# A Hyena, RWKV-7 and mixture-of-experts layer: the recurrent part in lockstep of four heads, issued in the order of a list scheduler

## The chip, the core and the metric

The program runs on one core of one Trainium2 chip. Time is device microseconds (us) of the whole program: one launch reads all inputs from memory and writes the output. The core has TensorE (PE; its weight loads are shown apart as PEld), VectorE (DVE), ScalarE (ACT), GpSimd (POOL) and SyncE (SP), which here only issues DMAs.

## The reference, cut to what matters

The layer works on 512 latent tokens (behind 256 context tokens) of 1024 channels, all in float32:

```
cols  = rmsnorm(x) * (1 + m[1]) + m[0]  @ w_in            # Hyena 1536, RWKV 1792, gates 2048 columns
y_hy  = hyena_branch(hy_cols) @ hy_proj                   # a long convolution
S <- S (diag(w) + a^T b) + v^T k ;  y = S r               # RWKV-7, 8 heads of 64, forwards and backwards,
                                                          # state carried over from the context tokens
y_rw  = (groupnorm(y_fwd + y_bwd) + bonus) * gate         # then @ rw_proj
mixed = (sigmoid(g_hy) * y_hy + sigmoid(g_rw) * y_rw) @ w_out
x     = x + m[2] * rmsnorm(mixed)
x     = x + m[5] * rmsnorm(experts(rmsnorm(x)))           # 16 experts, each takes its 64 best tokens
```

## The kernel before

The program runs through stages: modulation and norm, Hyena with all projections (to 322 us of the profiled execution), the **recurrent part** (322 to 784), the merge with the gates, output projection and router (784 to 939), and the experts, whose weights stream in from memory until the end.

In the recurrent part tokens are cut into chunks of 64. For one head and direction a batch is four chunks, and there are three: the context's (0) and the latents' two (1, 2). A head pair ("group", 4 of them) goes through these stages per batch: `pieces` (decays and scaled keys; two small float32r products "pus" per direction, L810, then a scan along time, L816), `scores` (L882), `inverses` and `levels` (the inverse of a triangular 64x64 matrix; the 16x16 blocks go through DRAM, L889 to L964, then small products, L973), `values` (values transposed on PE into UV, keys into BT), `steps` (L1043 to L1110) and at the end `epilogue`. In `steps` a chunk costs a chain: `p1` on PE (L1063, L1070), its copy X1 on DVE, `p2` on PE (L1076), the copy into UV, `p3` on PE (L1085), and the new state; the output `ya` (L1094, L1097) hangs beside it. The next chunk needs the state. Groups follow one another; two strings, ORD0 and ORD1, say how one group's steps are mixed with the preparation of the next, and the compiler's scheduler with priorities sets the final order.

Two kinds of other work stand between these products. The **gates** (L711 to L722) are 16 column tiles of `w_in`, each a 512 KB load and 16 matmuls of 256 tokens against the normalised input `hraw`, which is kept in SBUF. **Zeros** fill up: `pump` (L288) issues one matmul of zeros after `p1`, `p2` and `p3`, and each bank of `levels` first takes two (L941). The decay weights `ur` of a group come by one DMA on ACT's queue (the first group's early, "ahead", L686); ACT and POOL split them into `us`.

Each float32 matmul leaves two records in the trace, and counts below are of records. Raw weights pass through `raw_tile`s of 4 KB a partition, of which there are NRAW = 3; the gates use them, and the merge for `w_hy_proj`, `w_rw_proj` and `w_out`, where ACT (L212) and DVE (L216) split each into two parts.

## Time and profile before

| | us |
|---|---|
| median of 2 timed runs (1876.72 and 1878.56) | 1877.64 |
| span of the profiled execution, which is its own time too | 1886.6 |
| recurrent part in it | 322 to 784 |
| PE busy in the recurrent part | 444.13 of 462.00 |
| merge | 784 to 850 |

The page shows busy time of each engine over the span and in 40 slices; the stages above come from sums over windows of the trace and from its timeline. "PEclk" or the clock column is the share of full speed that TensorE was granted: 1.00 is 2.4 GHz, 0.50 is 1.2 GHz, and a mean between them says which part of the stretch each held.

### The profile page before, as it was taken

The numbers are of one execution on the slowest core, as the hardware profiler recorded it, in microseconds if no ns is written. First come the engines' busy times: TensorE is split into PE (matmuls) and PEld (weight loads), VectorE is DVE, ScalarE is ACT, GpSimd is POOL, SyncE is SP. The second block draws the span as 40 slices with busy tenths as digits, with TensorE's granted clock in tenths as the row PEclk, the third lists the DMA queues.
The fourth block names the chain that finished last, engine by engine and source line by source line (L and its number), as shares of the span: only waits on it lengthen the run. The fifth ranks groups of instructions, "written<-read, shape, count | busy, mean of one in ns | idle before, by whom it ended". The sixth has DMA issues, their size and how long they took to land.

```text
span 1886.6 us, 32798 instructions
## 1 busy us (share of the span) xinstructions
PE 1702.4 (90%) x14006; PEld 1107.5 (59%) x14006; DVE 681.9 (36%) x1520; ACT 434.5 (23%) x941; POOL 214.5 (11%) x255
## 2 busy tenths in 40 slices
PE   8898999999999999789599999889899898998985
PEld 3466786667666767668475545555455454554542
DVE  4765875867584742363500202002020020200203
ACT  3544531434453433333100000000000000000001
POOL 0534102422131300020000000000000000000000
PEclk5799999899999899999699999999999999999998
DMA  7255543433222221571799999999999999999995
GB/s 304 95 187 192 172 159 114 144 83 67 64 69 40 57 47 41 179 269 62 295 402 427 426 427 427 426 427 426 427 427 427 426 427 426 426 426 427 426 427 231
DMA packets 143292, 516.46 MB, mean 274 GB/s; under 512 B 83259, under 2 KB 87499, under 8 KB 118572
## 3 DMA queue, kind: packets, MB, share of 16 engines
q1 hardware_dynamic: 139824, 509.68, 68.8%
q10 hardware_dynamic: 3324, 4.70, 0.7%
q8 instruction: 110, 1.80, 0.4%
q14 instruction: 34, 0.28, 0.0%
HBM read 490.98 MB, written 23.36 MB: 273 GB/s over the span
## 4 chain that ended last, share of the span: by engine, by line
PE 39%; DMA 14%; DVE 3%; ACT 1%; issue 1%; POOL 0%; SPq 0%; DVEq 0%; ACTq 0%; POOLq 0%
PE ph L1425 17%; DMA exp_w<-in_exp_w 12%; PE py L1438 10%; PE px L1392 3%; PE pso L1460 3%; PE pht L249 1%; DVE hd L216 1%; PE po L1245 1%; PE po L1242 1%; PE po L1243 1%; ACT hT L212 1%; PE pl L1326 0%; PE pbq L1406 0%; PE pbp L1402 0%; DMA w_hy_proj<-in_hy_proj 0%
## 5 line engine op out<-in xcount | busy, mean ns | idle before, releaser
L1425 PE MATMUL ph<-exp_w,xe 128*64 128x256 f32 x4096 | 469.2, 380 | 26.7 <-DMA exp_w<-in_exp_w 26.7
L1425 PEld LDWEIGHTS ph<-exp_w,xe 128*64 128x64 f32 x4096 | 318.2, 137 | 194.8 <-issue 63.4
L216 DVE TENSOR_TENSOR hd<-ph,hd 128x256 f32<-128x256 f32 x64 | 27.2, 425 | 674.5 <-PE ph L1425 674.5
L1438 PE MATMUL py<-exp_w,hT 128*64 128x512 f32 x1024 | 236.8, 598 | 24.8 <-ACT hT L212 24.8
L1438 PEld LDWEIGHTS py<-exp_w,hT 128*64 128x64 f32 x1024 | 78.4, 136 | 138.7 <-issue 92.8
L719 PE MATMUL pgate<-hraw,w_gate 128*128 128x256 f32 x512 | 148.0, 409 | 0.7 <-ACT yo L212 0.3
L213 ACT ACTIVATE hd<-ph 128x256 f32<-128x256 f32 x64 | 24.5, 383 | 431.7 <-PE ph L1425 431.7
L719 PEld LDWEIGHTS pgate<-hraw,w_gate 128*128 128x128 f32 x512 | 90.6, 198 | 19.2 <-issue 3.8
L212 ACT ACTIVATE hT<-pht 128x256 f32<-128x256 f32 x64 | 24.5, 383 | 284.6 <-PE pht L249 284.6
L1392 PEld LDWEIGHTS px<-OH,xn 128*128 128x128 f32 x512 | 65.8, 197 | 23.4 <-issue 22.4
L1399 POOL COPY sel<-kcon 16x128 f32<-16x128 f32 x8 | 2.2, 283 | 609.4 <-PE pbq L1406 609.4
L1460 PE MATMUL pso<-ye,oT 128*128 128x512 f32 x128 | 68.7, 628 | 0.7 <-ACT ye L212 0.7
L1392 PE MATMUL px<-OH,xn 128*128 128x128 f32 x512 | 68.0, 282 | 0.9 <-DVE OH L223 0.9
L249 PE MATMUL pht<-kcon,hd 128*128 128x128 f32 x128 | 28.0, 301 | 36.1 <-DVE hd L216 35.9
L216 DVE TENSOR_TENSOR mo<-pso,mo 128x512 f32<-128x512 f32 x56 | 38.4, 691 | 39.3 <-PE pso L1460 39.3
L249 PEld LDWEIGHTS pht<-kcon,hd 128*128 128x128 f32 x128 | 12.9, 141 | 65.2 <-DVE hd L216 65.2
L882 PE MATMUL ps<-ar,bk 64*64 64x64 f32 (+1 forms) x512 | 46.5, 277 | 3.6 <-POOL bk L216 2.0
L882 PEld LDWEIGHTS ps<-ar,bk 64*64 64x64 f32 (+1 forms) x512 | 37.4, 177 | 16.5 <-POOL bk L216 5.0
L1443 DVE COPY ye<-py 64x512 f32<-64x512 f32 x16 | 11.1, 694 | 95.8 <-ACT ye L212 95.8
L216 POOL TENSOR_TENSOR mw<-mw 128x256 f32<-128x256 f32 x32 | 31.5, 1001 | 99.2 <-DVE mw L219 99.2
L288 PE MATMUL p<-zl 128*128 128x256 bf16 x140 | 40.0, 286 | 0.0
L212 ACT ACTIVATE sf<-st,fs 128x64 f32<-128x64 f32 x80 | 24.3, 341 | 49.6 <-DVE st L219 49.4
(396 smaller groups left out, 2549.7 us busy)
## 6 DMA issues: line engine op xcount, KB each, us to landing
exp_w<-in_exp_w SPq DMA_DIRECT2D x192, 2048.0 KB, 31.0
mw<-in_mod_w SPq DMA_DIRECT2D x48, 512.0 KB, 3.9
w_gate<-in_w_in SPq DMA_DIRECT2D x16, 512.0 KB, 4.9
w_h<-in_w_in SPq DMA_DIRECT2D x12, 512.0 KB, 4.1
w_c<-in_w_in SPq DMA_DIRECT2D x12, 512.0 KB, 5.6
g_d<-gt SPq DMA_DIRECT2D x16, 256.0 KB, 4.7
gg<-g_d SPq DMA_DIRECT2D x16, 256.0 KB, 5.5
w_o<-in_w_out SPq DMA_DIRECT2D x8, 512.0 KB, 5.3
```

The costliest lines, as they stand in the source:

```text
L212: return A.activation(out, in_, func, scale=scale, **kw)
L213: return A.activation(out, in_, func, bias=bias, scale=scale, **kw)
L216: e.tensor_tensor(out, a, b, op=op)
L249: TE.transpose(out, in_, ident[0:n, 0:n])
L288: mm(bk[:, 256:256 + NPW].rearrange("p (a b) -> p a b", b=P), zl, zw, start=True, stop=True)
L719: mm(pt[:, n:n + 256], w[:, k, :], hraw[:, k, n:n + 256], start=k == 0, stop=k == KD - 1)
L882: mm(pss[h][r, j * W:(j + 1) * W], BK[d](c)[HR[h], r], AR[d](c)[HR[h], 0:W], start=True, stop=True)
L1242: mm(pt, lhs[0][a], rhs[0][b], start=i == 0, stop=False)
L1392: mm(pt[:, k4 * P:(k4 + 1) * P], xn[:, n, k * P:(k + 1) * P], OH[:, n].rearrange("p a b -> p (a b)"), start=n == 0, stop=n == 3)
L1425: mm(ph[i][64 * hf:64 * hf + 64, 0:256], xe[:, k, 64 * e1:64 * e1 + 64], ws[i][:, k, hf * 256:(hf + 1) * 256], start=k == 0, stop=k == KD - 1)
L1438: mm(py[64 * dh:64 * dh + 64, :], hT_[:, i * P + 64 * hf:i * P + 64 * hf + 64], w2[:, 2 * hf + i, dh * 512:(dh + 1) * 512], start=b == 0 a ...
L1460: mm(pt, oT[:, n * P:(n + 1) * P], ye[:, dh * 512:(dh + 1) * 512], start=True, stop=True)
```

## The change

All engine calls of the recurrent part go through proxies of a class `Plan` and are only recorded. When the part is complete, `Plan.run` works out who depends on whom, gives each call a cost from a formula in the source, ranks it by the longest path behind it, schedules greedily per engine, and issues everything in that order under `manual_schedule`.

The stages are rewritten for two groups at a time (four heads, both directions): six units of work `(sg, bt)`, two groups `sg` alternating over three batches `bt`. An operation of `steps` is 8 matmuls of 64x64 in place of two times 4; the state update is two DVE operations. `scores` are 64x64 quadrants in two parts. No matmul of zeros is left in the part. `hraw` goes to DRAM (`h_d`) and comes back by quarters of 128 tokens; so each gate's weights are loaded four times, and a gate is 4 times 8 matmuls of 128 tokens. Values are transposed in the projection stage and stored (`vt_d`), and loaded by eight DMAs per unit. All four `us` are made at the start through one buffer, `gs`. NRAW is 2.

```diff
-NP1, NP2, NP3, NPW = 1, 1, 1, 256
-NRAW = 3
+NRAW = 2
+NMS, NAR, NBK, NUV, NBT = (3, 2), 3, 1, 2, 2
...
+class Plan:
+    def add(self, engine, what, f, a, k):
...
+            if what == "transpose" or min(rows, cols) > 64 or single:
+                place, t = None, 0.2 if what == "transpose" else size * (0.00055 if single else 0.00175) + 0.02
+            else:
+                place, t = (lhs.offset // lhs.ap[0][0], out.offset // out.ap[0][0]), 0.116 * size / 64
...
+        if what == "dma_start":
...
+            cost, lat = 0.07, 2.2 + size / (180e3 if run >= 512 else 60e3)
+        elif engine == "gpsimd":
+            cost, lat = 0.1 + 0.0023 * size, 0.1
+        elif engine == "scalar":
+            cost, lat = 0.15 + 0.0009 * size, 0.15
...
+    def run(self, tc):
...
+        for o in reversed(ops):
+            o["rank"] = o["cost"] + max((o["lat"] + ops[j]["rank"] for j in o["succ"]), default=0.0)
...
+                    o = min(rs, key=lambda o: (max(t, o["from"]), -o["rank"]))
...
+        with tc.manual_schedule():
+            for o in order:
+                for f, a, k in o["calls"]:
+                    f(*a, **k)
...
+                        vt = hp.tile([P, 6, P], F32, tag="vt", name=f"vt{m}")
+                        for a, b in ((0, 4), (4, 6)):
...
+                                transpose(pv[:, (i - a) * P:(i - a + 1) * P], cz[:, i * P:(i + 1) * P])
...
-            # the RWKV part's first group starts from these
-            ahead = raw_tile("ur0")[:, 0:2 * CT], raw_tile("k3c0")[:, 0:3 * CT]
-            A.dma_start(out=ahead[0], in_=I["ups"][0].rearrange("p i d f -> p (i d f)"))
...
-            w = filler[0](f"w_gate{i}").rearrange("p (k f) -> p k f", k=KD)
-            SY.dma_start(out=w, in_=w_in[o // P])
-            pt = pfl(f"pgate{i}")
-            for n in (0, 256):
-                for k in range(KD):
-                    mm(pt[:, n:n + 256], w[:, k, :], hraw[:, k, n:n + 256], start=k == 0, stop=k == KD - 1)
...
+            us = []
+            for g in range(4):
+                ur = buf("gs", [P, 2, 2, P])
+                A.dma_start(out=ur, in_=I["ups"][g])
+                u_ = rp.tile([P, 2, 2, P], F32R, name=f"us{g}")
+                act(u_, ur, AF.Copy)
...
+            def gates(i, q, h):
+                pt = sfl(f"pgate{q}{i}")
+                for n in range(4):
...
+                    w = turns("raw", raw_tile, NRAW).rearrange("p (k f) -> p k f", k=KD)
+                    SY.dma_start(out=w, in_=w_in[o // P])
+                    for k in range(KD):
+                        mm(pt[:, P * n:P * n + P], w[:, k, :], h[:, k, :], start=k == 0, stop=k == KD - 1)
...
+            for u in units:
+                pieces(u)
+                scores(u, 0)
+                inverses(u)
...
+            plan.run(tc)
```

ACT at the start of the recurrent part. `yo` is the last copy of the Hyena stage, `w1` and `ta` take the decays from `pus`, `E3` follows the scan. Before:

```order
L213 ACTIVATE cz3_2224<-pcl3_2225,par_67 128x512
L212 ACTIVATE yo3_2351<-pyo3_2346 128x256
L212 ACTIVATE us0_2388<-ur0_2280 128x512
L213 ACT_TABLE_LOAD
L213 ACTIVATE w1000_2396<-pus_2386,par_67 128x256
L213 ACTIVATE ta000_2397<-pus_2386,par_67 128x256
L213 ACTIVATE E3000_2416<-gs000_2405 128x256
```

With the change, where `gs_0` is the buffer that all four loads share with the first scan (`E3` reads it):

```order
L333 ACTIVATE yo3_2412<-pyo3_2407 128x256
L889 DMA gs_0_2439<-in_ups 128x512
L333 ACTIVATE us0_2441<-gs_0_2439 128x512
L889 DMA gs_0_2439<-in_ups 128x512
L313 ACT_TABLE_LOAD
L313 ACTIVATE w1_0_2470<-psmm_0_2472,par_67 128x256
L333 ACTIVATE us1_2446<-gs_0_2439 128x512
L313 ACTIVATE ta_0_2471<-psmm_0_2472,par_67 128x256
L889 DMA gs_0_2439<-in_ups 128x512
L333 ACTIVATE us2_2451<-gs_0_2439 128x512
L333 ACTIVATE us3_2456<-gs_0_2439 128x512
```

One load that lay ahead of the part has become four in turn, each behind the reader of the one before, and all four stand ahead of the first `E3`. (A second pair of `w1` and `ta` and the fourth DMA, which only repeat, are left out.)

PE in one step of the last group. `M`, `X`, `BT`, `AR` and `ar` are the prepared matrices, `st` the state, `psfl` and `pgate` a gate. Before:

```order
L1070 MATMUL p1313_7676<-st3120_7667,ar301_6490 64x64 x2
L1070 MATMUL p1313_7676<-st3121_7671,ar311_6527 64x64 x2
L288 LDWEIGHTS zl_61
L288 MATMUL p1313_7676<-zl_61 128x256
L719 MATMUL pgate13_8188<-hraw_173,w_gate13_8186 128x256 x2
L1076 MATMUL p2313_7687<-X1313_7675,xf1_2381 64x64 x4
```

With the change:

```order
L313 MATMUL psfl_0_2526<-hh_0_2525,raw_0_2527 128x128 x4
L313 MATMUL psst_1_2495<-st1_1_2508,AA_2_2509 64x64 x8
L313 MATMUL psya_0_2518<-AR_0_2510,st1_0_2507 64x64 x8
L313 MATMUL psfl_0_2526<-hh_0_2525,raw_1_2528 128x128 x4
L313 MATMUL psst_0_2494<-X1_0_2493,xf1_2436 64x64 x8
L313 MATMUL psfl_0_2526<-hh_0_2525,raw_1_2528 128x128 x4
```

Between `p1` and `p2` stood a matmul of zeros and two of a gate; now there stand matmuls of the other pair of groups and four of a gate at half the width.

SP at the stretch where a group's inverse comes back from DRAM. Before:

```order
L930 DMA X_d1_2374<-rb30_6109 64x16x16
L931 DMA X_d1_2374<-rt30_6110 64x16x16
L964 DMA X30_6267<-X_d1_2374 32x16x32 x4
L889 DMA N_d2_2373<-M320_6673 64x8x64
L722 DMA g_d_72<-gt10_8139 128x512
L715 DMA w_gate13_8186<-in_w_in 128x1024
```

With the change:

```order
L313 DMA g_d_72<-stg_0_2529 128x4x128
L313 DMA X_d1_2430<-rb_0_2482 128x16x16
L313 DMA X_d1_2430<-rt_0_2483 128x16x16
L313 DMA raw_0_2527<-in_w_in 128x1024
L313 DMA XX_0_2489<-X_d1_2430 32x16x32 x8
L313 DMA raw_1_2528<-in_w_in 128x1024
```

A gate's load, which waits for a raw buffer, now stands ahead of the eight loads that bring the inverse back.

## Rows read from the trace of the kernel before

**Rows 1.** The page's first line.

```profile
span 1886.6 us, 32798 instructions
```

**Rows 2.** Sums over windows: stretch, length, engines' busy time, granted clock, DMA share.

```profile
200.00:305.00 105.00, 103.19 (x505) 80.53 (x504) 76.17 (x96) 33.50 (x50) 15.41 (x15) 1.00 0.50 165
322.00:784.00 462.00, 444.13 (x6292) 316.69 (x6290) 265.14 (x773) 190.39 (x490) 104.57 (x152) 0.96 0.30 74
784.00:850.00 66.00, 52.28 (x210) 40.95 (x211) 41.64 (x47) 23.03 (x27) 13.96 (x9) 0.91 0.77 270
1228.00:1821.00 593.00, 534.49 (x3702) 305.40 (x3698) 72.33 (x159) 39.54 (x95) 3.20 (x4) 1.00 1.01 427
```

**Rows 3.** The same of one stretch of the recurrent part.

```profile
339.00:357.00 18.00, 15.63 (x76) 10.57 (x75) 12.79 (x36) 6.82 (x18) 7.16 (x9) 0.62 0.20 51
```

**Rows 4.** Timeline there: start, duration, line, count, idle before, its releaser.

```profile
341.27 0.68 PE L882 MATMUL ps<-ar,bk 64*64 64x64 f32 x28 [1.75 <-POOL bk L216]
```

**Rows 5.** Timeline of PE: 256-column gates, later 128-column products.

```profile
773.94 7.07 PE L719 MATMUL pgate<-hraw,w_gate 128*128 128x256 f32 x32
...
1029.62 2.17 PE L1392 MATMUL px<-OH,xn 128*128 128x128 f32 x18
1031.72 3.65 PE L1438 MATMUL py<-exp_w,hT 128*64 128x512 f32 x16
```

**Rows 6.** Timeline of PE, steps of the last group.

```profile
748.92 0.34 PE L1094 MATMUL ya<-M,UV 128*64 128x64 f32 x4
749.19 0.33 PE L1097 MATMUL ya<-ar,st 64*64 64x64 f32 x4
...
750.36 0.45 PE L1070 MATMUL p<-st,ar 64*64 64x64 f32 x8
750.74 0.28 PE L288 MATMUL p<-zl 128*128 128x256 bf16 x1
750.86 1.03 PE L719 MATMUL pgate<-hraw,w_gate 128*128 128x256 f32 x4
```

**Rows 7.** Timeline of PE, scores and levels.

```profile
333.90 0.69 PE L882 MATMUL ps<-ar,bk 64*64 64x64 f32 x32
334.52 0.38 PE L810 MATMUL pus<-lh,us 128*128 128x256 f32 x1
...
399.17 0.38 PE L941 MATMUL lvs<-zl 128*128 128x256 bf16 x2
399.48 0.45 PE L973 MATMUL lvs<-PP,X 32*32 32x32 f32 x32
...
656.52 1.16 PE L882 MATMUL ps<-ar,bk 64*128 64x128 f32 x8
```

**Rows 8.** Costliest groups of PE: busy, mean ns of one, idle before.

```profile
L249 PE MATMUL pv<-kcon,vz 128*64 128x128 f32 x48 | 9.0, 292 | 0.0
```

**Rows 9.** DMA issues: queue, count, KB each, median us from issue to landing.

```profile
w_gate<-in_w_in SPq DMA_DIRECT2D x16, 512.0 KB, 4.9
ur<-in_ups ACTq DMA_DIRECT2D x4, 256.0 KB, 3.7
```

**Rows 10.** Timeline of all engines, start of the recurrent part.

```profile
323.27 0.62 ACT L212 ACTIVATE us<-ur 128x512 fp32r<-128x512 f32 x1
...
324.47 2.19 POOL L216 TENSOR_TENSOR us<-ur,us 64x256 fp32r<-64x256 f32 x2
...
327.15 0.69 DVE L816 TENSOR_TENSOR_SCAN gs<-kcon,w 128x256 f32<-128x256 f32 x1
```

**Rows 11.** Timeline of SP's queue, the inverse's way back.

```profile
403.60 4.16 SPq L964 DMA_DIRECT2D X<-X_d  x8
```

**Rows 12.** The chain of waits, in the merge.

```profile
814.57 5.27 DMA w_o<-in_w_out
819.86 1.07 ACT wh_o L212
820.95 1.47 DVE wl_o L216
```

More of the change, by code (lines that the diff above doesn't have):

```diff
@@ L262, in program @@
     g_d = tc.dram_tile([16, P, T], F32, name="g_d")
+    h_d = tc.dram_tile([4, P, KD, T // 4], F32, name="h_d")
+    vt_d = tc.dram_tile([4, S, P], F32, name="vt_d")
     u_d = tc.dram_tile([4, P, T], F32, name="u_d")
@@ L743, in program @@
                 SY.dma_start(out=x_d.rearrange("m a s t -> (m a s t)").rearrange("(p f) -> p f", p=P), in_=zx[:, 0:f])
-            xfs = [rp.tile([P, 2, 4, C], F32, name=f"xf{i}") for i in range(NX)]
+            xfs = [rp.tile([P, 2, 2, 4, C], F32, name=f"xf{i}") for i in range(2)]
             for xf in xfs:
@@ L904, in inverses @@
+            def inverses(u):
+                n = 64
+                nm = u["nm"]
+                nb = buf("nb", [P, BASE, BASE])
+                rb = buf("rb", [P, BASE, BASE])
+                rt_ = buf("rt", [P, BASE, BASE])
+                pr = buf("pr", [P, 512])
+                pa = buf("pa", [P, 64])
+                SY.dma_start(out=nb, in_=blocks(u["N_d"], 0, 32))
                 F_, B_ = slice(0, n), slice(n, 2 * n)
@@ L945, in levels @@
[L945 to L953 removed]
+                for i in range(1, 4):
+                    contract(at(rb, 16 * i, [68, 4], [1, i]), (4, i, i),
+                             at(rb, 0, [68, 4], [1, i], [16, i]), at(rt_, i, [68, 4], [0, i], [16, i]))
@@ L1112, in epilogue, with values @@
-            def epilogue(q):
-                g, bs = q["g"], q["bs"]
-                y = rq.tile([P, T], F32, tag=TYE, name=f"y{g}")
-                act(y, q["ya"], AF.Copy)
+                            act(XF[r, :, a, :, FC[1 - a]], p3(pz)[r], AF.Copy)
+            def values(u):
+                nm, sg, bt, BK = u["nm"], u["sg"], u["bt"], u["BK"]
+                UV = u["UV"] = [buf(f"UV{h}", [P, 2, 2, 4, C], NUV) for h in range(2)]
+                BT = u["BT"] = buf("BT", [P, 2, 2, 4, P], NBT)
+                for h in range(2):
+                    G.memset(UV[h][HR[h]], 0.0)
+                for gi in range(2):
+                    src = vt_d[2 * sg + gi].rearrange("(c t) p -> t c p", t=C)
+                    for d in range(2):
+                        cs = seqs[d][4 * bt:4 * bt + 4]
+                        for h in range(2):
+                            s_ = src[:, min(cs):min(cs) + 4, 64 * h:64 * h + 64]
+                            SY.dma_start(out=UV[h][HR[1 - h], gi, d], in_=s_[:, ::-1] if d else s_)
+                for gi in range(2):
+                    for d in range(2):
+                        pt = sbank("sc", 2, f"pb{nm}{gi}{d}")
+                        for j in range(4):
+                            transpose(pt[:, j * P:(j + 1) * P], BK[:, gi, d, 3 - j if d else j].rearrange("p a t -> p (a t)"))
+                        act(BT[:, gi, d].rearrange("p j t -> p (j t)"), pt, AF.Copy)
+                        cut()
@@ L1142, in epilogue @@
+                mm(pg, gup, sg, start=True, stop=True)
+                cut()
                 stt(y, pg, 0.5, y, ALU.mult, ALU.mult)
@@ L1185, in program @@
-            run(ORD0, (0, False))
-            for g in range(4):
-                pair[0], pair[1] = pair[1], None
-                run(ORD1, (g + 1, g == 3))
-            for i in range(16):
-                gates(i)
+            units = [dict(sg=n % 2, bt=n // 2, nm=f"{n % 2}{n // 2}", N_d=N_d[n % 2], X_d=X_d[n % 2], xf=xfs[n % 2]) for n in range(6)]
+            for u in units:
+                pieces(u)
+                scores(u, 0)
+                inverses(u)
+                if u["bt"]:
+                    scores(u, 1)
+                values(u)
+                levels(u)
+                steps(u)
+                if u["bt"] == 2:
+                    for g in (2 * u["sg"], 2 * u["sg"] + 1):
+                        epilogue(g)
@@ L1191, in program @@
+            for q in range(4):
+                hh = buf("hh", [P, KD, T // 4])
+                SY.dma_start(out=hh, in_=h_d[q])
+                for i in range(0, 16, 4):
+                    gates(i, q, hh)
+            plan.run(tc)
             ts(V, modA[:, 1, :, 0], mcol[:, 3, :, 0], 1.0, None, ALU.add)
```

796 lines of the change are left out of this document (410 added, 386 removed).

## The prediction

> **What bounds the kernel now.** I read the sums over windows first. The profiled execution spans 1886.6 us [rows 1], 9.0 us or 0.5% above the median of the timed runs, 1877.64; I form differences on it and take them off the median. In the experts the transfers fill the stretch (share 1.01, 427 GB/s), and nothing there changes [rows 2]; the experts' weights have to wait for the end of the recurrent part, so what that part gains or loses reaches the end one for one. In the recurrent part, 322 to 784 us, PE is busy for 444.13 of 462.00 us at a mean clock of 0.96, with DVE at 265.14, ACT at 190.39, POOL at 104.57 and a DMA share of 0.30 [rows 2]. So the part is bound by PE's queue of work, with 18 us of gaps, and an edit there is priced by PE time first. The mean of 0.96 lies between the two levels 1.2 and 2.4 GHz (0.50 and 1.00): 8% of the part ran at the lower one, which cost about 18 us. The timeline shows where: PE waited 1.75 us for POOL's keys at 341.27 [rows 4], and the 18 us around it ran at a mean of 0.62 [rows 3]. That is 76% of them at the lower level, and a loss of half of 13.7 us, 6.8 us. I call that **one cold stretch** below.
>
> **The change, part by part.** All counts are records of the trace.
>
> *Gates.* Before, 32 records of 256 columns took 7.07 us, 0.221 each [rows 5]; 512 of them make 113.1 us. After, there are 1024 of 128 columns. The nearest row is the experts' 128x128x128 product: 18 records between 1029.62 and 1031.72 us, 0.117 each [rows 5]. 1024 x 0.117 = 119.8, so **+6.7 us**.
>
> *Steps.* Both kernels issue 1984 records. Eight of the chain's start 0.38 us apart (750.36 to 750.74), 0.0475 each; four of the output's `ya` take 0.27 us (748.92 to 749.19), 0.0675 each [rows 6]. Before, 1472 x 0.0475 + 512 x 0.0675 = 104.5. After, the output's are in runs of eight on all four quadrants too, and I give them the chain's price: 1984 x 0.0475 = 94.2, **-10.3 us**. The lower bound on the gain is nothing.
>
> *Scores.* Quadrants of 64x64: 32 records in 0.62 us, 0.0194 each; the 64x128 form: 8 in 1.16, 0.145 each [rows 7]. Before, 256 of either, 42.1 us. After, 1280 quadrants, 24.8 us: **-17.3 us**.
>
> *Zeros.* 140 pumps at 0.12 us (750.74 to 750.86) [rows 6] are 16.8 us, and 60 pairs before the levels at 0.31 (399.17 to 399.48) [rows 7] are 18.6: **-35.4 us** if what stands behind them can start sooner. Nothing, if PE would wait for DVE in that time anyway.
>
> *Transposed values.* 48 records, 9.0 us busy as listed [rows 8], 5.6 by the 0.117 of the 128-column row [rows 5]: **-5.6 us** here. The same transposes come back in the projection stage, where PE is busy for 103.19 of 105.00 us [rows 2] and nothing covers them: **+6 us** there, with the stores of `h_d` and `vt_d` on a DMA share of 0.50 [rows 2], which I cost at nothing. Between 2 us, if the few gaps take them, and 9.
>
> Products of `levels`, `pus`, keys' transposes and epilogues stay. PE's work in the part falls by 6.7 - 10.3 - 17.3 - 35.4 - 5.6 = **-62 us**.
>
> *The start.* Before, ACT copied the preloaded `ur` at 323.27 in 0.62 us, POOL's two subtractions took 2.19, and the first scan ran at 327.15 [rows 10]. After, nothing is loaded ahead, and four loads go through one buffer, which the first scan needs as well. A round is a load of 3.7 us [rows 9], the copy of 0.62 and the 2.19 of POOL [rows 10]: 6.5 us. From 323.3 the fourth ends near 349.3, and the scan runs some 22 us later. What PE can do until then is eight pairs of `pus` at about twice 0.38 [rows 7] and a few 128-column gate matmuls behind their 4.9-us loads [rows 9], about 7 to 8 us of work. I take **+14 us**, between 10 and 22.
>
> *The clock without zeros.* No row shows the part without them. Upper bound: a cold stretch in every one of the six units' preparations, 6 x 6.8 = 41, and one more in the start, 48. Lower bound: nothing, since four gate records stand in each gap of a step and a pair of groups has the other one's products in between, as the order shows. The rows nearest to it are those at 341.27, where zeros did not prevent the fall either [rows 3, 4]. I take two more cold stretches, **+12 us** rounded down for the work done in them.
>
> *Waits.* Order is now fixed by costs written down in the source, and 0.07 us is what it plans for a DMA on SP. The eight that bring an inverse back kept SP for 4.16 us, 0.52 each [rows 11]; there are 48 of these and some 200 other DMAs on that queue, behind which inverses, keys and gate loads stand. Of the gate loads the order puts one ahead of the inverse's; when its raw buffer is still being read, the inverse waits, and with it the levels and the next steps of that pair. Against it, half as many rounds of the chain (24 of four heads in place of 48 of two). Zero to 25 us; I take **+12 us**. The gate loads by themselves are no bound: a pair of buffers turning over in 4.9 us of load [rows 9] and 1.9 of 16 matmuls gives 3.4 us for each of 64, 218 us in a part twice as long.
>
> *The merge.* The chain of waits there shows a raw buffer's round: load 5.27, ACT's half 1.07, DVE's 1.47 [rows 12], 7.8 us. Over three buffers that is 2.6 us per 512 KB, over two 3.9; for the sixteen loads of 512 KB in the merge's matrices 1.3 x 16 = 21 us more if it is all exposed. PE is busy for 52.28 of 66.00 us there [rows 2], so much of it is hidden: **+8 us**, between 2 and 21.
>
> The sum: -62 + 14 + 12 + 12 = -24 in the recurrent part, + 6 in the projections, + 8 in the merge: -10 us. 1877.64 - 10 = **1868 us**.
>
> **The rivals.**
>
> *Faster.* All of the 62 us is gained, and neither waits nor a colder clock are added, since gate matmuls come in pieces of four wherever a gap is planned: -62 + 12 + 4 + 5 = -41, so about **1837 us**; 1832 at best. For it: PE was the bound for 96% of the part [rows 2]. Against it: the 18 us of gaps and 18 us of lower clock are waits, which a new order need not remove and may add to.
>
> *Slower: the clock falls in the gaps.* The place is the preparation of each unit, where a pair's scores wait for DVE and POOL, and its levels for the way through DRAM. A 512-KB load (4.9 us [rows 9]) now brings only 16 x 0.117 = 1.9 us of gate work, where before it brought 32 records, 7.07 us [rows 5]; so a run of gates cannot bridge a long wait at full clock. With ten cold stretches in place of two the part costs 68 - 12 = 56 us more: **1924 us**. Gain and loss balance at one or two more cold stretches than I took; it takes seven more to be slower by 2%. For it: the stretch at 341.27 [rows 3, 4]. Against it: it was a single wait of 1.75 us, and in the middle of the part the order before seldom left PE without work.
> The Trainium skill, page "TensorE: Matmul & The Clock Gate", section "HAM oscillation — how this bites in real kernels", speaks against this change: where the matmuls on one loaded tile take less time than the wait for the next, the array falls back to half rate at each tile. By that rule this rival would be the likeliest; the trace agrees as to the cause at 341.27 and shows no stretch with gates this thin.
>
> *No gain: zeros sat in waits.* If PE would have waited for DVE during the zeros, the 35 us come back as gaps, of which 12 are in the sum: 1868 + 23 = **1891 us**. For it: a zero pair stands right where the product behind it needs DVE's result [rows 7]. Against it: gates stand there too.
> The Trainium skill, page "Perfetto Trace Analysis", section "Identifying the Most-Contended Engine", says that matmul busy time is a poor measure of how full PE is, and that the busy share of weight loads is a good one. Here that share is 316.69 of 462.00 [rows 2], not 96%, which would leave room for waits like these; the trace does not decide it.
>
> **How the numbers follow.** Chances: the forecast 0.46, faster 0.24, slower 0.20, no gain 0.10. The bounds of 2%, about what a measurement of this kernel can tell from no change, lie at 1840.1 and 1915.2. The forecast's own terms run from -62 + 10 + 2 + 2 = -48 to -52 + 22 + 48 + 25 + 21 + 9 = +73, and not all ends come together: 1840 to 1900. The range takes in the faster rival to 1832 and the slower one to 1925, and leaves out the rest, 2 in 10. Faster by over 2%: 0.20 of that rival and 0.04 of the forecast. Slower: 0.16 of its rival, 0.05 of the rest. Within: 0.55.
>
> **What would show it.** In the window of the recurrent part: gate records 0.117 apart, scores under 30 us, PE busy about 60 us less, the part some 440 us long with a mean clock not under 0.92; the first scan around 348; loads and splits of the merge in twos. A mean clock of 0.85 or less with many waits of 2 us or more before scores and levels would be the slower rival; a part near 420 us the faster one. I would be wrong altogether if 128-column gate matmuls took much more than 0.117, or if the part's end waited for something other than PE: a single queue on SP, or a chain of one unit with no gates left to put in its gaps.

## The result, and the profile after

The changed kernel took 1927.4 us (1924.27 and 1930.53) against 1877.64: a ratio of 1.0263, 95% interval 1.022 to 1.0305. Forecast were 1868, range 1832 to 1925: the direction was wrong, and the time is near what the "slower" rival gave (1924), though, as the table shows, not where that rival puts the loss. The page's first line, which answers to [rows 1]:

```profile
span 1928.7 us, 34429 instructions
```

That is 42.1 us more than before; the timed medians differ by 49.8, since the profiled execution of before lay 9 us above its median; in which stretch it lost them is not known, so a difference below can be off by as much. Where the 42.1 us are is read from four points on PE's timeline of both kernels: the end of the Hyena stage (its last product), the first scores, the last output product of a step, and the first product of the merge.

| | before | changed | difference | forecast |
|---|---|---|---|---|
| end of the Hyena stage | 322.9 | 344.0 | +21.1 | +6 |
| from there to the first scores (start) | 11.0 | 42.4 | +31.4 | +14 of PE's time |
| to the last output product (middle) | 430.3 | 409.7 | -20.6 | -38 |
| to the merge's first product | 25.7 | 35.5 | +9.8 | +8, whole merge |
| from there to the end | | | +0.4 | |

The sums over these last three stretches, before (columns as in [rows 2]):

```profile
322.90:333.90 11.00, 10.10 (x44) 7.16 (x41) 7.86 (x18) 5.28 (x12) 8.59 (x16) 1.00 0.91 297
333.90:764.20 430.30, 417.11 (x6171) 295.89 (x6170) 251.60 (x746) 176.95 (x467) 94.72 (x136) 0.96 0.28 66
764.20:789.90 25.70, 16.02 (x76) 13.00 (x76) 5.48 (x10) 9.22 (x13) 1.27 (x1) 0.93 0.58 185
```

and of the changed kernel:

```profile
344.00:386.40 42.40, 15.14 (x60) 11.78 (x60) 7.39 (x12) 10.42 (x21) 15.96 (x21) 0.61 0.57 176
386.40:796.10 409.70, 340.42 (x7125) 294.66 (x7124) 206.72 (x457) 118.79 (x290) 82.12 (x104) 0.86 0.56 144
796.10:831.60 35.50, 13.20 (x73) 9.95 (x73) 8.79 (x16) 10.83 (x15) 2.53 (x2) 0.66 0.48 153
```

In the middle PE is busy for 340 us in place of 417: PE's work did fall. But its gaps grew from 13 to 69 us and the mean clock fell from 0.96 to 0.86. In the start PE is busy for 15 of 42 us. By the table the miss, from -10 to +42.1 us, is some 17 us in the middle, 17 in the start, 15 in the Hyena stage and 2 in the merge. Next, PE's timeline (start, duration), which answers to [rows 5 to 7]:

```profile
776.83 0.68 PE L313 MATMUL psst<-st,AA 64*64 64x64 f32 x16
777.35 0.63 PE L313 MATMUL psya<-AR,st 64*64 64x64 f32 x16
...
786.11 1.16 PE L313 MATMUL psfl<-hh,raw 128*128 128x128 f32 x8
787.20 0.69 PE L313 MATMUL psst<-UV,BT 128*64 128x64 f32 x16
...
797.58 1.95 PE L313 MATMUL psfl<-hh,raw 128*128 128x128 f32 x16
799.36 0.95 PE L313 MATMUL pssc<-kcon,rz 128*128 128x2 f32 x8
```

64 scores quadrants take 1.09 us (412.06 to 413.15), 0.017 each (forecast 0.0194); sixteen of a step's products 0.52 us, 0.0325 each (0.0475 forecast); gates 0.136 in runs of eight, 0.111 in a run of sixteen (0.117). So steps and scores cost less than priced, and gates in short runs a little more. What PE waits for (the waits view, start to merge: total, times, longest):

```profile
PE psfl L313 <- DMA raw<-in_w_in: 16.9, 9, 4.5
PE psmm L313 <- ACT w L313: 15.8, 6, 9.2
PE psmm L313 <- POOL us L337: 10.2, 1, 10.2
PE pslv L313 <- DMA XX<-X_d: 10.1, 9, 3.5
```

Before, the largest entry of this view inside the part was 2.6 us; these four are 53. Of them 26 us lie in the middle (12.4, 3.8 and 10.1 of the first, second and fourth) and the rest in the start; the middle's 69 us of gaps are these and many smaller ones.

### The profile page after: what moved, and what is told of

It is laid out like the page before. It is cut to its first block, busy times and chain, and to the rows that moved or that the text cites. A ratio compares the mean times of both kernels' runs of the same rounds, so it can differ in the third digit from the quotient of the medians.

```text
span 1928.7 us, 34429 instructions
## 1 busy us (share of the span) xinstructions
PE 1635.7 (85%) x14998; PEld 1112.1 (58%) x14998; DVE 636.2 (33%) x1232; ACT 385.5 (20%) x783; POOL 209.1 (11%) x230
## 4 chain that ended last, share of the span: by engine, by line
PE 60%; DMA 19%; DVE 9%; issue 4%; POOL 3%; ACT 3%; SPq 1%; ACTq 0%; DVEq 0%; POOLq 0%
PE ph L328 17%; DMA exp_w<-in_exp_w 12%; PE py L328 9%; PE psfl L313 5%; PE pcl L328 3%; PE px L328 3%; PE pso L328 3%; PE psst L313 3%; PE po L328 2%; PE pssc L313 2%; DMA mw<-in_mod_w 2%; PE pslv L313 1%; DMA raw<-in_w_in 1%; PE pht L370 1%; DVE hd L337 1%
## 5 line engine op out<-in xcount | busy, mean ns | idle before, releaser
L313 PE MATMUL psfl<-hh,raw 128*128 128x128 f32 x1024 | 163.9, 313 | 22.0 <-DMA raw<-in_w_in 16.9
L313 PEld LDWEIGHTS psfl<-hh,raw 128*128 128x128 f32 x1024 | 142.8, 217 | 36.5 <-issue 13.5
L370 PE MATMUL pht<-kcon,hd 128*128 128x128 f32 x128 | 28.0, 300 | 35.7 <-DVE hd L337 35.5
L337 DVE TENSOR_TENSOR mo<-pso,mo 128x512 f32<-128x512 f32 x56 | 38.4, 690 | 39.3 <-PE pso L328 39.3
L313 PE MATMUL psmm<-lh,us 128*128 128x256 f32 x48 | 21.4, 446 | 30.4 <-ACT w L313 15.8
L313 DVE TENSOR_TENSOR M<-pssc,kcon 128x256 f32<-128x256 f32 x80 | 29.6, 416 | 28.5 <-PE pssc L313 28.3
L340 DVE SCALAR_TENSOR_TENSOR mw<-mw,sc,mw 128x256 f32<-128x256 f32 x64 | 28.0, 488 | 18.4 <-DMA mw<-in_mod_w 16.6
L328 PE MATMUL phy<-ha,wh_h 128*128 128x512 f32 x96 | 30.2, 446 | 2.3 <-ACT wh_h L333 2.3
```

Of the source, the lines that this page charges most:

```text
L313: f(*a, **k)
L328: return TE.matmul(*a, **k)
L337: e.tensor_tensor(out, a, b, op=op)
L340: V.scalar_tensor_tensor(out, a, s, b, op0=op0, op1=op1)
L370: TE.transpose(out, in_, ident[0:n, 0:n])
```

## The experiments

All ratios are to the kernel before, timed beside each run. The columns are the end of the Hyena stage, the length of the start and of the middle, from each one's profiled execution.

| run | time, us | ratio, 95% interval | Hyena end | start | middle |
|---|---|---|---|---|---|
| changed kernel, again | 1932.95 | 1.0293, 1.0271 to 1.0316 | 347.4 | 42.3 | 406.7 |
| before, two raw buffers | 1890.16 | 1.0068, 1.0036 to 1.0100 | 309.3 | 9.7 | 437.0 |
| three raw in the projections | 1919.33 | 1.0216, 1.0180 to 1.0252 | 337.0 | 42.6 | 406.1 |
| `ur` ahead | 1918.76 | 1.0214, 1.0173 to 1.0255 | 341.1 | 35.2 | 402.5 |
| a quarter of the gate loads | 1903.71 | 1.0121, 1.0079 to 1.0164 | 336.8 | 41.6 | 377.5 |
| no transposes in the projections | 1909.00 | 1.0167, 1.0137 to 1.0198 | 327.4 | 41.8 | 405.0 |
| gates of 256 tokens | 1918.44 | 1.0223, 1.0201 to 1.0245 | 342.5 | 44.6 | 394.0 |
| zeros put back | 1933.35 | 1.0298, 1.0267 to 1.0329 | 345.7 | 42.0 | 406.8 |
| transposes one column later | 1915.56 | 1.0194, 1.0149 to 1.0239 | 337.7 | 41.1 | 401.0 |
| gate loads on POOL's queue | 1918.02 | 1.0214, 1.0173 to 1.0255 | 339.3 | 40.4 | 403.6 |
| gate loads on ACT's queue | 1911.08 | 1.0171, 1.0132 to 1.0210 | 337.9 | 38.4 | 399.7 |
| five edits | 1896.85 | 1.0090, 1.0060 to 1.0120 | 326.7 | 40.8 | 388.6 |
| five edits, loads on ACT | 1896.06 | 1.0102, 1.0063 to 1.0140 | 325.3 | 41.9 | 394.0 |
| four edits, loads on ACT | 1895.22 | 1.0100, 1.0054 to 1.0147 | 326.3 | 32.1 | 394.7 |
| no gates | 1870.79 | 0.9949, 0.9922 to 0.9976 | 338.5 | 33.2 | 354.6 |
| no wait for the inverse | 1902.87 | 1.0143, 1.0096 to 1.0189 | 341.8 | 47.6 | 381.0 |

Eight kernels whose projections the edit leaves alone ended the Hyena stage between 336.8 and 345.7 us, the changed kernel itself at 344.0 and 347.4. So that one point moves by some 10 us between profiles, and a difference of it under that is not read. Most of that scatter lies ahead of the last `pc<-kcon,acc` on PE, which starts between 200.6 and 210.7 us in these ten; from there to the stage's end they take 134.8 to 137.6 us, and this length can be read:

| | last `pc<-kcon,acc` | from there to the stage's end |
|---|---|---|
| before | 202.1 | 120.9 |
| before, two raw buffers | 188.5 | 120.9 |
| changed kernel, and again | 206.5, 210.7 | 137.5, 136.8 |
| three raw in the projections | 204.8 | 132.2 |
| no transposes in the projections | 205.2 | 122.2 |
| transposes one column later | 212.4 | 125.3 |
| the runs of five, five and four edits | 203.0, 202.0, 203.1 | 123.7, 123.3, 123.2 |

The middle scatters too: the six kernels that leave it alone (changed, again, three raw, `ur` ahead, the two on transposes) range from 401.0 to 409.7 us.

### The Hyena stage

*The kernel before with two raw buffers* in place of three, alone:

```diff
-NRAW = 3
+NRAW = 2
```

> The kernel before with two raw buffers in place of three, nothing else. In the changed kernel the last matmul of the Hyena stage ends at 344.0 us, before at 322.9: 21 us late. Theory R: two raw buffers hold up the projections, whose weights pass through them too; then this run's Hyena stage ends near 340 and it takes 1893 to 1903 us, or more if its recurrent part suffers as well. Rival V: the 21 us come from the values' transposes and the stores of h_d and vt_d, which this run does not have; then its Hyena stage ends at 323 to 326 and it takes 1876 to 1886 us, the rest being the merge.

It took 1890.16 us, 0.7% more: above what rival V allowed and below theory R's range. Its Hyena stage ended at 309.3 us, earlier than in the kernel before (322.9), all of it ahead of `pc<-kcon,acc`; the stretch behind that is 120.9 us in both. The middle was 7 us longer, and the stretch to the merge's first product took 33.5 us in place of 25.7. Two raw buffers do not hold up the end of the Hyena stage there, so theory R falls as the cause of the 21 us.

*Three raw buffers in the projections of the changed kernel:*

```diff
-            w = raw_tile(f"w_{name}").rearrange(...)
+            w = wp.tile([P, 1024], F32, tag="rawc", bufs=3, name=f"w_{name}").rearrange(...)
```

> The changed kernel with three raw buffers of their own for the weights of the projections, the two others as they were. Theory R: the Hyena stage ends at 324 to 330 in place of 344, and the time falls by 14 to 20 us, to 1907 to 1913. Rival V (transposes and stores): the stage still ends at 340 or later, 1922 to 1930.

1919.33, and the stage ends at 337.0, neither 330 nor 340. By the ratios (1.0216 against 1.0263 and 1.0293) it is 9 to 14 us less. The stage's end is inside its own spread; the stretch behind `pc<-kcon,acc`, 132.2 us, is 2.6 us under the shortest of the ten, so these buffers hold a few us of it.

*No transposes of the values there*, stored as they come:

```diff
-                            for i in range(a, b):
-                                transpose(pv[:, (i - a) * P:(i - a + 1) * P], cz[:, i * P:(i + 1) * P])
-                            act(vt[:, a:b].rearrange("p n c -> p (n c)"), pv[:, 0:(b - a) * P], AF.Copy)
-                        SY.dma_start(out=vt_d[m - 8].rearrange("(n p) c -> p n c", p=P), in_=vt)
+                        SY.dma_start(out=vt_d[m - 8].rearrange("(n p) c -> p n c", p=P), in_=cz.rearrange("p (n c) -> p n c", c=P))
```

> The changed kernel without the transposes of the values in the projection stage: the values are stored as they are, so the recurrent part reads values in a wrong order and the output is not the reference's; 24 transposes (4.4 us of PE) and 8 copies on ACT are left out, the stores and loads stay. Theory V: PE stands behind these transposes, which wait for DVE and for ACT; the Hyena stage ends 8 us or more earlier than in the unchanged kernel of this call, and the time falls by 8 to 15 us. Rival: only their 4.4 us of work goes, 3 to 6 us.

24 us less than the changed kernel timed beside it (1909.0 against 1932.95), more than either theory said, and the stage ends at 327.4. Behind `pc<-kcon,acc` it is 14.6 us shorter (122.2 against 136.8): the 4.4 us of work cost more than three times as much. Two pieces of PE's timeline show one place where. The changed kernel, measured again, behind the first key column:

```profile
210.66 0.50 PE L328 MATMUL pc<-kcon,acc 128*128 128x1 f32 x4
215.13 2.93 PE L328 MATMUL pn<-kk,kcon 128*128 128x256 f32 x4 [3.97 <-ACT kk L334]
217.07 3.97 PE L328 MATMUL pcl<-ha,wh_c 128*128 128x512 f32 x8
220.88 2.03 PE L328 MATMUL pcl<-ha,wl_c 128*128 128x512 f32 x8
```

PE has the squares `pn` next in its order and waits 3.97 us for ACT's `kk`; the products behind it then start at the lower clock (3.97 us for eight, 2.03 for the next eight; the granted clock is 0.54 from 215.1 to 220.9). Without the transposes, at the same place:

```profile
205.21 0.50 PE L328 MATMUL pc<-kcon,acc 128*128 128x1 f32 x4
207.42 2.99 PE L328 MATMUL pcl<-ha,wh_c 128*128 128x512 f32 x8 [1.71 <-DVE cz L340]
210.21 2.21 PE L328 MATMUL pn<-kk,kcon 128*128 128x256 f32 x4
```

the next column's products stand ahead of `pn`, which finds its data ready. So the transposes change the order of the stage, not only its work.

*The transposes one column later*, all work kept, with a third buffer for the columns `cz`:

```diff
-                cz = hp.tile([P, S], F32, tag="cz", bufs=2, name=f"cz{m}")
+                cz = hp.tile([P, S], F32, tag="cz", bufs=3, name=f"cz{m}")
...
+                while late:
+                    late.pop(0)()
...
+                        late.append(turned)
```

> The changed kernel with each value column's transposes issued behind the next column's products (three cz buffers in place of two); all work stays. Without the transposes the Hyena stage had ended 20 us earlier (327.4 against 347.4) and the time had fallen by 24 us, though they are 4.4 us of PE work. Theory V2: their place costs, since PE stands behind columns that DVE is still mixing and the squares behind them wait for ACT; then this run's stage ends by 335 and it takes 1912 to 1921 us. Rival: the work itself, copies on ACT and banks costs; the stage ends after 340 and the time stays within 5 us of 1930.

1915.56, where theory V2 had 1912 to 1921; the stage ends at 337.7, not by 335, but `pc<-kcon,acc` came at 212.4, later than in any other profile. From it to the stage's end, the changed kernel measured again and this run (columns as in [rows 2]):

```profile
210.66:347.45 136.79, 126.72 (x582) 97.67 (x580) 87.08 (x115) 38.04 (x60) 17.96 (x18) 0.95 0.43 139
212.42:337.72 125.30, 121.41 (x582) 94.24 (x580) 87.37 (x115) 36.92 (x60) 18.36 (x18) 1.00 0.47 151
```

The same 582 records take 11.5 us less, with 6 us less of gaps and the clock at 1.00. Together with the three raw buffers (in the runs of four and five edits below) the stretch takes 123.2 to 123.7 us, against 120.9 before. So of the 21 us some 16 lie behind that product; 13 of them are order and buffers, and come back with all the work in place. How they split between the transposes' place and the third `cz` buffer stays open.

### The start

*`ur` loaded ahead*, all four, into the two raw buffers:

```diff
+            ahead = [raw_tile(f"ups{i}") for i in range(2)]
+            for g in range(4):
+                A.dma_start(out=ahead[g // 2][:, 512 * (g % 2):512 * (g % 2) + 512], in_=...)
-                ur = buf("gs", [P, 2, 2, P])
-                A.dma_start(out=ur, in_=I["ups"][g])
+                ur = ahead[g // 2][:, 512 * (g % 2):512 * (g % 2) + 512].rearrange(...)
```

> The changed kernel with all four ur loaded ahead, into the two raw buffers, during the end of the Hyena stage. Theory S: the four loads in turn through gs hold the first scan (373.9); without them it runs at about 356 and the time falls by 12 to 18 us, to 1909 to 1915. Rival: the start waits for the Hyena stage's buffers and the chain of decays anyway; the scan is not before 366 and the time falls by less than 6 us.

In the changed kernel the start looks like this (all engines and queues; [rows 10] before):

```profile
339.86 7.23 SPq L832 DMA_DIRECT2D u_d<-yy  x3
349.73 0.33 ACTq L889 DMA_DIRECT2D gs<-in_ups  x1
352.37 0.63 ACT L333 ACTIVATE us<-gs 128x512 fp32r<-128x512 f32 x1 [7.93 <-DMA gs<-in_ups]
...
354.90 0.33 ACTq L889 DMA_DIRECT2D gs<-in_ups  x1
...
371.66 0.63 ACT L333 ACTIVATE us<-gs 128x512 fp32r<-128x512 f32 x1 [4.78 <-DMA gs<-in_ups]
372.37 1.51 POOL L337 TENSOR_TENSOR us<-gs,us 64x256 fp32r<-64x256 f32 x2 [3.90 <-ACT us L333]
373.91 1.23 DVE L313 TENSOR_TENSOR_SCAN gs<-kcon,w 128x512 f32<-128x512 f32 x1 [12.67 <-POOL us L337]
```

In the trace nothing of the part begins until the Hyena stage's last store has left its buffers: SP issues the last of three `u_d` stores at 347, and ACT the first load of `ur` at 349.73. Then each load waits for the subtraction before it, in rounds of 5 to 9 us, and the scan runs at 373.91, 29.9 us behind the stage; before, at 327.15, it was 4.2 us behind. With the loads ahead:

```profile
346.58 2.19 ACT L333 ACTIVATE us<-ups 128x512 fp32r<-128x512 f32 x4 [4.97 <-DMA u_d<-yy]
...
357.38 1.22 DVE L313 TENSOR_TENSOR_SCAN gs<-kcon,w 128x512 f32<-128x512 f32 x1
...
366.17 1.27 POOL L313 TENSOR_TENSOR BK<-ta,k 128x512 f32<-128x512 f32 x1 [2.98 <-DVE ta L313]
372.56 3.78 PE L313 MATMUL psfl<-hh,raw 128*128 128x128 f32 x16 [6.71 <-DMA raw<-in_w_in]
376.27 1.64 PE L313 MATMUL pssc<-AA,BK 64*64 64x64 f32 x64
```

the scan runs at 357.38, 16.3 us behind the stage, as theory S said, 13.6 us sooner than in the changed kernel; but the start is only 7 us shorter, and the time, 1918.76, is 9 to 15 us below the changed kernel's by the ratios, not at theory S's 1909 to 1915. Of the 19 us from the scan to the first scores 10 are preparation: the last keys `BK` are ready at 367.44. For the other 9 PE stands at a gate that the fixed order puts ahead of the scores: it waits 6.71 us for that gate's weights and then multiplies. In the changed kernel the same gate holds the scores for 3.1 us (383.3 to 386.4). Without gates (below) the first scores run 7.4 us behind the scan, and the start is 33.2 us. So the hole has three parts: the release of the buffers (to 346.6 here), the loads of `ur`, and gates ahead of the scores.

### The middle: loads, clock, or chain

*A quarter of the gate loads:*

```diff
+                    if not q:
                         SY.dma_start(out=w, in_=w_in[o // P])
```

> The changed kernel with the gates' weights loaded in the first quarter of the tokens only (16 loads in place of 64); the later quarters multiply whatever lies in the raw buffers, so the gates of 384 tokens are not the reference's. All matmuls stay. Theory Q: the gate loads hold up PE, by their own waits (16.9 us listed) and by standing ahead of the inverses on SP; then the time falls by 20 to 45 us, to 1882 to 1907. Rival C (the clock falls while the preparation's chain of DVE, ACT, POOL and DRAM runs, whatever the loads do): 0 to 10 us, 1917 to 1928.

```profile
378.40:755.90 377.50, 314.27 (x7078) 270.55 (x7077) 207.89 (x457) 117.96 (x289) 77.22 (x104) 0.92 0.39 90
```

1903.71: by the ratios 27 to 32 us below the changed kernel, as theory Q said. The middle is 377.5 us, though in a profiled execution 12 us shorter than the other three of this run. What such a load does is seen on SP in the last unit of the changed kernel:

```profile
747.69 0.97 SPq L313 DMA_DIRECT2D X_d<-rt  x1
748.75 2.15 SPq L313 DMA_DIRECT2D raw<-in_w_in  x1
753.12 4.05 SPq L313 DMA_DIRECT2D XX<-X_d  x8
754.16 2.08 PE L313 MATMUL psfl<-hh,raw 128*128 128x128 f32 x8 [4.49 <-DMA raw<-in_w_in]
SPq L313 <- DMA X_d<-rt: 2.2, 1, 2.2
```

PE waits 4.49 us for a gate's weights, whose buffer the gate before it read until 749.7, with no other gate left whose weights are there. The eight loads of the inverse stand behind that load on SP, but what SP waits for last ahead of them, 2.2 us (the last line, from its waits between 747.5 and 753.5), is the landing of their own store `X_d`; here the gate's load did not hold them up.

*Gates of 256 tokens*, 32 loads, the ring AR with two buffers:

```diff
-            for q in range(4):
-                hh = buf("hh", [P, KD, T // 4])
+            for q in range(2):
+                hh = buf("hh", [P, KD, T // 2])
```

> The changed kernel with gates of 256 tokens: each weight tile is loaded twice in place of four times (32 loads) and brings 16 matmuls of 256 columns; to make room the ring AR has two buffers in place of three. Theory Q (gate loads hold up PE; leaving three quarters of them out had brought some 24 us): the time falls by 10 to 18 us, to 1908 to 1917. Rival: longer gate pieces and the shorter ring cost as much as the loads give, 1920 to 1930.

1918.44, 14.5 us below the changed kernel timed beside it, the gain expected, though the time is 1.4 us above theory Q's range. But the waits for the inverse grew from 10.1 us to

```profile
PE pslv L313 <- DMA XX<-X_d: 29.9, 18, 10.5
```

12.5 us of them after the gates had run out, 45 us before the last output product: fewer loads, and another wait in their place.

*Gate loads on POOL's queue, and on ACT's:*

```diff
-                    SY.dma_start(out=w, in_=w_in[o // P])
+                    G.dma_start(out=w, in_=w_in[o // P])
```

> The changed kernel with the 64 gate loads issued from POOL's queue in place of SP's; everything else is as it was, and the list scheduler plans with it. Theory H (head of line): gate loads that wait for a raw buffer stand ahead of the inverses' way through DRAM on SP, and PE then waits for XX and, behind it, without gates; moved away, the middle stretch shrinks from 407 us to 385 or less and the time to 1900 to 1915. Rival: what costs is the loads' rate through two buffers, wherever they are issued: the stretch stays over 397 us and the time at 1920 to 1940.

> The same with the gate loads on ACT's queue. Theory H: a gain as on POOL's queue, or less, since ACT's copies into UV then stand behind loads that wait for a raw buffer: 1905 to 1925. Rival (rate of the loads): no gain, and ACT's waits add to the steps: 1930 to 1950.

SP's waits for buffers that gate products are reading, in the middle of the changed kernel (386 to 796 us; total, times, longest):

```profile
SPq L313 <- PE psfl L313: 121.5, 42, 12.2
```

with the loads on POOL's queue they are 3.1 us. So SP was freed of some 118 us of standing behind gate loads. The times fell (1918.02 and 1911.08, under the rival's ranges), yet the middle is 403.6 and 399.7 us long, over the 397 that the rival allowed, and inside or 1.3 us under the range of kernels that leave it alone (401.0 to 409.7). Some 8 and 9 us of the gain lie in the Hyena stage (its end at 339.3 and 337.9 against 347.4), which these edits don't touch and which scatters. So a gain in the middle from another queue is not shown, and theory H explains little: the number of loads costs more than their queue.

*Zeros put back*, recorded and scheduled with the rest:

```diff
+                    zeros(p1, 256, 2)
                     V.tensor_copy(X1, four(p1))
...
                 pp = plv(0)
+                zeros(pp, 0, 2)
```

> The changed kernel with matmuls of zeros put back, recorded with the rest: two after each p1, p2 and p3, and two ahead of each product of the levels, some 200 in all, about 27 us at full clock. Theory C (the clock falls because nothing fills the gaps): the mean clock of the middle stretch rises from 0.86 to 0.92 or more, and the time falls by 5 to 15 us. Rival W: the gaps are waits of several us for loads and for other engines, which two zeros cannot bridge; the clock stays under 0.90 and the time grows by 5 to 25 us.

The middle of the changed kernel timed beside it, and with zeros:

```profile
389.70:796.40 406.70, 336.99 (x7125) 291.70 (x7124) 207.67 (x457) 118.61 (x290) 81.12 (x104) 0.87 0.57 145
```

```profile
387.70:794.50 406.80, 347.09 (x7309) 285.41 (x7308) 209.81 (x457) 118.87 (x290) 77.52 (x104) 0.93 0.57 143
```

The clock rose from 0.87 to 0.93, as theory C said; the time, which either theory had moving by 5 us or more, did not (1933.35 against 1932.95), nor did the middle (406.8 against 406.7). But zeros are work too: 200 records, by the 0.12 us of [rows 6] an estimated 24 us of PE, and in the trace the copies and the state's update behind `p1`, `p2` and `p3` wait for them 44 times. PE's gaps did not grow, they shrank by 10 us. Whether the higher clock gives nothing, or gives what the zeros cost, this run does not separate. That the clock follows the waits at least in part is seen where waits go and no zeros come: it is 0.92 with a quarter of the gate loads, and 0.92 without the wait for the inverse.

*No gates at all:*

```diff
-                for i in range(0, 16, 4):
-                    gates(i, q, hh)
             plan.run(tc)
+            for i in range(16):
+                SY.dma_start(out=g_d[i], in_=bs[0])
```

> The changed kernel without gates: no gate loads and no gate matmuls (some 120 us of PE at full clock, 64 loads); the 16 stores write other data, so the output is not the reference's. Theory L (the chain of preparation, inverse and steps sets the length of the middle stretch, gates only fill it): the stretch from the first scores to the last output product, 407 us, stays over 350 us even without 120 us of PE work. Rival P (PE's queue of work sets it): it falls by about the work left out and its share of the lower clock, to 250 to 300 us.

```profile
371.70:726.30 354.60, 241.54 (x6180) 193.02 (x6180) 206.74 (x458) 108.81 (x274) 80.66 (x105) 0.70 0.34 76
```

With some 120 us of PE work left out the middle still takes 354.6 us, PE busy for 241.5 of them at a mean clock of 0.70. Theory L holds: the chain of preparation and steps needs some 350 us by itself, at this clock; how long it would take at full clock is not shown. The gates and their loads add the other 52 us, less than half of their work.

*Levels that don't wait for the inverse:*

```diff
-                nm, M, x_d = u["nm"], u["MA"], u["X_d"]
+                nm, M, x_d = u["nm"], u["MA"], X_d[2]
```

> The changed kernel with levels that read zeros from DRAM in place of the inverse's blocks, so that they do not wait for it; the inverse is computed and stored all the same, all other work stays, and the output is not the reference's. Theory L: the way through DRAM and DVE is the long link of the chain; without it the middle stretch falls from 407 to 385 us or less, and the time to 1890 to 1912. Rival: the scheduler had hidden the inverse behind the other pair's steps; under 8 us.

```profile
389.40:770.40 381.00, 316.71 (x7109) 274.63 (x7108) 206.54 (x458) 118.32 (x290) 78.10 (x104) 0.92 0.58 152
```

1902.87 us, by the ratios 22 to 28 below the changed kernel, and a middle of 381.0 us in place of 406.7: the way of the inverse through DVE and DRAM is a link of that chain and holds some 26 us of it, with the order that the plan then makes.

### Do the causes add up?

*Five edits* (a_combo): transposes later, three raw buffers, `ur` ahead, gates of 256 tokens, and

```diff
-                SY.dma_start(out=y_d[g], in_=y)
+                A.dma_start(out=y_d[g], in_=y)
```

> The changed kernel with five edits: transposes one column later, three raw buffers of their own in the projections, ur loaded ahead, gates of 256 tokens (32 loads), and the stores of y_d on ACT's queue so that the merge's weights don't stand behind them. If the single effects add up (10 to 20, some 8, 12, 14, and 5 to 8 us from 1930): 1870 to 1882 us, as fast as the kernel before. Rival: the start and the middle share one wait (the inverses' way through DRAM, 29.9 us of waits for XX with gates of 256), so the sum falls short: 1885 to 1905.

The same with the gate loads on ACT's queue (a_combog), and that without the gates of 256 tokens (a_combo4):

> The five edits of a_combo and the gate loads on ACT's queue. If SP's order still costs there (27.6 us of waits for XX), 1878 to 1890; if the loads, halved already, no longer stand in the way, 1892 to 1900.

> The same without the gates of 256 tokens: 64 loads of gate weights on ACT's queue, 128 columns, three AR buffers. In a_combo the gates were used up 44 us before the last step, with nothing left to fill the last unit; here they last longer. If that matters more than the loads: 1875 to 1888; if the loads do: 1892 to 1905.

1896.85, 1896.06 and 1895.22: about two thirds of the loss are back, and all three stay 0.9 to 1.0% slower than the kernel before. Each time the slower of the two expectations was right: the single effects do not add up. One reason is in the start of the first of them, with `ur` ahead and yet 40.8 us long:

```profile
358.85 8.31 PE L313 MATMUL psfl<-hh,raw 128*128 128x256 f32 x24 [9.30 <-DMA hh<-h_d]
```

The keys are ready at 352.9 and the scores run at 367.5: PE stands at gates ahead of them in its order, waits for their input and multiplies 24 records. That is not the shared wait for the inverse that the rival named. The last of the three:

```profile
326.30:358.40 32.10, 13.24 (x60) 10.27 (x60) 7.39 (x12) 9.62 (x20) 15.57 (x21) 0.68 0.58 179
358.40:753.10 394.70, 332.31 (x7126) 287.76 (x7124) 207.00 (x457) 118.81 (x291) 78.18 (x105) 0.87 0.58 151
753.10:789.70 36.60, 13.23 (x73) 9.95 (x73) 8.76 (x16) 10.94 (x15) 2.52 (x2) 0.66 0.46 150
```

Against before (11.0, 430.3 and 25.7): the Hyena stage is 3 us late, the start 21 us longer, the tail 11, and the middle 36 shorter. (These lengths are of its profiled execution, 4.5 us below its median; that of before lay 9 us above: the lengths tell where, the ratios how much.) The stores of `y_d` on ACT's queue did not shorten the tail (36.6 against 35.5 us); its wait is this, in the changed kernel:

```profile
806.54 10.33 SPq L313 DMA_DIRECT2D y_d<-Y  x2
...
818.81 0.63 ACT L333 ACTIVATE yh<-yr 128x512 fp32r<-128x512 f32 x1 [8.60 <-DMA y_d<-Y]
...
826.81 1.00 SPq L1342 DMA_DIRECT2D w_hy_proj<-in_hy_proj  x2
830.45 1.06 ACT L333 ACTIVATE wh_hy_proj<-w_hy_proj 128x1024 fp32r<-128x1024 f32 x1 [3.72 <-DMA w_hy_proj<-in_hy_proj]
831.56 0.29 PEld L328 LDWEIGHTS ppr<-yh,wh_hy_proj 128*128 128x128 f32 x1 [18.71 <-ACT wh_hy_proj L333]
SPq L1342 <- DMA yr<-u_d: 3.3, 1, 3.3
```

The last two groups' epilogues end together, SP issues the last `y_d` by 816.9, and ACT begins on the merge's inputs `yr` when that store has left the part's buffers (818.81). Between 818 and 826 two more `yr` pass through the two raw buffers ahead of the weights: SP waits for them (the last line, from its waits between 796 and 832) before it issues the first weights at 826.81, which reach PE at 831.56. With one group at a time the last epilogue had gates beside it until 781.0. A third raw buffer was not tried here; in the kernel before, this stretch took 33.5 us with two and 25.7 with three, so the buffers may hold part of the 9.8.

Not tried at all: the new stages in the compiler's order, or the old stages in the planned order. What the lockstep costs and what the fixed order costs is not told apart.

## Why the prediction was wrong

- **What bounds the part.** The step that failed is the first one: "bound by PE's queue of work", so that an edit "is priced by PE time first". That fits before, where PE was busy for 417 of the middle's 430 us. PE's busy time in the middle did fall, by 77 us, but of the forecast 62 us only 21 came off the middle, since its gaps grew by 56 us, where *Waits* allowed for 25 at most. The middle had become bound by its chain for the most part: without any gates it still takes some 355 of 410 us. My 12 us of waits and 12 of clock were worked out as if PE still set the time, and the start and the transposes were priced by PE's own time too.
- **Gates, steps, scores.** The prices 0.117, 0.0475 and 0.0194 us were measured as 0.111 to 0.136, 0.0325 and 0.017. Not at fault.
- **Zeros.** Forecast -35.4 us if what stands behind them starts sooner. Put back, they cost nothing net of the higher clock that they brought, which fits the "no gain" rival on this term.
- **The clock.** The slower rival's mark, a mean of 0.85 or less with long waits, was seen (0.84 over start and middle, 0.86 in the middle), and its time was nearly right by luck: with its 56 us for cold stretches the part should have been 32 us longer than before, and start and middle together are 11 us longer; the rest of the loss is elsewhere. What the clock costs the middle stays open. The rows that I took for zeros that did not prevent the fall [rows 3, 4] say nothing on them: none stands on PE between 323.2 and 375.7 us in that trace. The Trainium skill, page "TensorE: Matmul & The Clock Gate", section "HAM oscillation — how this bites in real kernels", says that where the matmuls on one loaded tile take less time than the wait for the next, the array falls back to half rate at each tile. The trace agrees in part: PE waited for 9 of the 64 loads (16.9 us), and with three quarters of the loads left out the clock of the middle was 0.92 in place of 0.86.
- **Gate loads.** They "by themselves are no bound", at 218 us for 64 loads: not contradicted as a rate, wrong as a price. Leaving three quarters of them out is worth 27 to 32 us.
- **The Hyena stage.** Mis-sized, +6 against +21.1, of which some 16 us lie behind `pc<-kcon,acc` and the rest within the scatter ahead of it. I priced 48 records of transposes, where the change issues 24 there, and not what they do to the order of a full PE. That two raw buffers serve the projections too, I had left out; it holds a few us.
- **The start.** Mechanism right, size not: 42.4 us in place of 11. The four rounds took 24 us (26 forecast), but from 349.7, when the Hyena stage's buffers come free, and not from its end; so the scan lies 25.7 us further behind the stage than before (22 forecast). From the scan to the first scores it is 12.5 us in place of 6.7, 3.1 of them a gate ahead of the scores. And the work that PE did meanwhile, for which I took off 7 to 8 us, was 5 us more than before. The release of the buffers and the stretch behind the scan were left out.
- **The merge.** +9.8 us before its first product and +0.4 behind, against +8: near in number by luck. The rounds of weights that I priced, behind the first product, cost nothing; the hole ahead of it is, by the trace, the late epilogues, the release of their buffers, and `yr` in the two raw buffers.

## What to carry to other kernels

Taking work off the busiest engine is priced by that work only down to the next bound: ask how long the dependent chain would take with all filler removed, which is one run (here 355 of 410 us). Twice the width with half the chains made each product cheaper here, and left holes of 31 and 10 us more at the first and the last unit. Work added to a full engine that runs in a fixed order cost here what stood behind it (4.4 us of transposes cost 15), and a gate whose weights are late holds up the chain that stands behind it in that order. Filler that raised the clock from 0.87 to 0.93 gave back no more than it cost.

## What was not expected of the hardware

Sixteen 64x64 products spread over all four quadrants start 0.0325 us apart where runs of eight before took 0.0475. With the gates left out, the mean granted clock of the middle was 0.70 although PE was busy for 241.5 of 354.6 us. And a stage of unchanged instructions ended between 336.8 and 347.4 us in ten profiles, while its last 135 to 138 us repeated within 3 us.
